# A rotary-embedding score kernel whose TensorE program becomes a loop, with explicit semaphores and whole stores

## The chip, the cores and the metric

The kernel runs on one core of a Trainium2 chip. The metric is the device time of one execution in microseconds (us); the time of a kernel is the median of its runs. A profile is one execution taken by the hardware profiler, and its span is a little shorter than the time (798.6 us here, for a time of 800.01 us).

A core has a matrix engine (TensorE, "PE" in the profile, with its weight loads as "PEld"), a vector engine (VectorE, "DVE"), a scalar engine (ScalarE, "ACT"), GpSimd ("POOL") and SyncE ("SP"), which here only issues transfers. Sixteen transfer (DMA) engines move data between the chip's memory (DRAM) and the core's on-chip memory. Matrix products land in PSUM and are copied from there by ScalarE or VectorE.

## The reference

Queries and keys of 16 batches, 512 positions, 16 heads and 64 dimensions are rotated by position, and then each head's scores are formed over all pairs of positions. All is float32.

```python
q, k: (16, 512, 16, 64);  cos, sin: (512, 32)

q1, q2 = q[..., :32], q[..., 32:]
q_rot = concatenate([q1 * cos - q2 * sin,  q1 * sin + q2 * cos], axis=-1)
# k_rot in the same way
scores = einsum('bshd,bthd->bsht', q_rot, k_rot)      # (16, 512, 16, 512)
```

The output has 268.4 MB, the inputs 67.1 MB: this kernel mostly writes.

## The kernel before

There are 64 steps, four for each batch. A step makes the scores of 128 query positions (one of four residues, `C = 4`) against all 512 key positions for the 16 heads, 4 MB, in a stage buffer `st` of which there are three, and stores it with one transfer.

In a step, eight score pairs (two heads each) go through TensorE into one of three PSUM buffers, and ScalarE evicts each pair into the stage buffer. Between them TensorE transposes rotated queries and keys of later steps through two PSUM banks, and VectorE does the rotation and half of the copies.

```python
    def scores(i, p, st):
        ps = ps_s_pool.tile([P, 2, S], fp32, tag="ps_s", name="ps")      # three buffers
        ...
        for r in range(2):
            po, rh = ps[:, r, :], rhs[64 * r : 64 * r + 64, :]
            nc.tensor.matmul(
                out=po, lhsT=lhs[64 * r : 64 * r + 64, :], rhs=rh, start=True, stop=True
            )
        ...
        nc.scalar.copy(out=so, in_=si)                                  # evicts into st
        ...
        elif b > 0 and p == HP - 1:
            store(i, st)
```

All stores but two are one transfer of 128 rows of 32 KB. Those of the steps 56 and 63 (`NST - 8` and `NST - 1`) are cut in three: most heads for all 128 rows, then the last two or three heads for 116 rows and for 12 rows.

```python
    def store(i, st):
        o = o_v[i // C, i % C]
        if i not in (NST - 8, NST - 1):
            nc.sync.dma_start(o, st)
            return

        h = H - 2 if i < NST - 1 else H - 3
        nc.sync.dma_start(o[:, :h], st[:, :h])
        nc.sync.dma_start(o[:116, h:], st[:116, h:])
        nc.sync.dma_start(o[116:, h:], st[116:, h:])
```

The main loop is a Python loop: every step's instructions stand in the program one by one. Waits between engines and for transfers are put in by the framework from the use of the tiles.

```python
        for i in range(C, NST):
            ...
            st = stage_pool.tile([P, H, S], fp32, tag="stage", name="st")
            for p in range(HP):
                scores(i, p, st)
                if p not in tr:
                    continue
                if tr[p][0] == "q":
                    run(dve[:1])
                    dve = dve[1:]
                    transposed(*tr[p], nc.vector.tensor_copy)
                else:
                    transposed(*tr[p], nc.scalar.copy)
            run(dve)
            if i % C == C - 2:
                load("q", i // C + 2)
            elif i % C == C - 1:
                load("k", i // C + 3)
```

The first four steps (`i < C`) are special: they work on batch 0 head by head, on inputs that come in four smaller loads into the third stage buffer (`early`), and store in pieces of 1 MB, so that the stores start early.

Of the kernel before, what the change touches and what calls it, by code (L numbers as in the profile page):

```python
# [7 lines left out]


@with_exitstack  # L10
def kernel(
# [15 lines left out]
    P = 128  # L27
# [3 lines left out]
    G = H // C  # L31

    const_pool = ctx.enter_context(tc.tile_pool(name="const", bufs=1))
    in_pool = ctx.enter_context(tc.tile_pool(name="in", bufs=2))
    part_pool = ctx.enter_context(tc.tile_pool(name="part", bufs=1))
    kt_pool = ctx.enter_context(tc.tile_pool(name="kt", bufs=2))
    qt_pool = ctx.enter_context(tc.tile_pool(name="qt", bufs=2))
    stage_pool = ctx.enter_context(tc.tile_pool(name="stage", bufs=3))
    ps_s_pool = ctx.enter_context(tc.psum_pool(name="ps_s", bufs=3))
    ps_t_pool = ctx.enter_context(tc.psum_pool(name="ps_t", bufs=2))  # L40

# [7 lines left out]
    ident = const_pool.tile([P, P], fp32, name="ident")  # L49
    cos_t = const_pool.tile([P, C, HD], fp32, name="cos_t")  # L50
    sin_t = const_pool.tile([P, C, HD], fp32, name="sin_t")
    ss_t = const_pool.tile([P, C, 2, HD], fp32, name="ss_t")
    ss_v = ss_t.rearrange("p c x j -> p c (x j)")

    st_first = [stage_pool.tile([P, H, S], fp32, tag="stage", name="st") for _ in range(2)]
    early = stage_pool.tile([P, 2 * C * H * D], fp32, tag="stage", name="early")
    units = {}
    used = [0]  # L60

    def load_units(which, head, heads):
        n = C * heads * D
        t = early[:, used[0] : used[0] + n].rearrange("p (c e) -> p c e", c=C)
        used[0] += n
        src = dram[which][0, :, :, head : head + heads, :]
        nc.sync.dma_start(t.rearrange("p c (h d) -> p c h d", d=D), src)
        for h in range(0, heads, G):
            units[which, (head + h) // G] = t[:, :, D * h : D * (h + G)]

    batches = {}

    def load(which, b):

        if b >= B:
            return
        t = in_pool.tile([P, C, H * D], fp32, tag=which + "_in", name=which + "_sb")
        batches[which, b] = t
        nc.sync.dma_start(t.rearrange("p c (h d) -> p c h d", h=H), dram[which][b])

    def rope(which, n):


        part = part_pool.tile([P, H * D], fp32, tag="part", name="part")
# [9 lines left out]
        else:  # L94
            x = batches[which, n // C][:, n % C]
# [7 lines left out]
        xs, xc = x.rearrange(sv, **k2), x.rearrange(sv, **k1)  # L103

        def products():
            nc.vector.tensor_tensor(pv, xs, ss, op=mult)  # L106
            nc.vector.tensor_tensor(xc, xc, cs, op=mult)  # L107

        def sums():
            for y, z in adds:  # L110
                nc.vector.tensor_tensor(y, y, z, op=add)  # L111
# [3 lines left out]
    kT = {}  # L115
    qT = {}

    def transposed(which, n, g, copy):


        bank = ps_t_pool.tile([P, 4, P], fp32, tag="ps_t", name="bank")
        for x in range(4):
            if n < C:
                src = units[which, n][:, x, P * g : P * (g + 1)]
            else:
                src = batches[which, n // C][:, n % C, P * (4 * g + x) : P * (4 * g + x + 1)]
            nc.tensor.transpose(bank[:, x, :], src, ident)  # L127
        src = bank
        if which == "q":
            if n not in qT:  # L130
                qT[n] = qt_pool.tile([P, HP, P], fp32, tag="qT", name="qT_t")
            dst = qT[n][:, 4 * g : 4 * g + 4, :]
        else:
            b = n // C
            if b not in kT:
                kT[b] = kt_pool.tile([P, HP, S], fp32, tag="kT", name="kT_t")
            if n < C:
                dst = kT[b][:, 2 * n + g].rearrange("p (t c) -> p t c", c=C)
                src = bank.rearrange("p c t -> p t c")
            else:  # L140
                dst = kT[b][:, 4 * g : 4 * g + 4, P * (n % C) : P * (n % C + 1)]
        copy(out=dst, in_=src)  # L142

    def store(i, st):
        o = o_v[i // C, i % C]
        if i not in (NST - 8, NST - 1):
            nc.sync.dma_start(o, st)
            return

        h = H - 2 if i < NST - 1 else H - 3  # L150
        nc.sync.dma_start(o[:, :h], st[:, :h])
        nc.sync.dma_start(o[:116, h:], st[:116, h:])
        nc.sync.dma_start(o[116:, h:], st[116:, h:])

    def scores(i, p, st):

        ps = ps_s_pool.tile([P, 2, S], fp32, tag="ps_s", name="ps")
        b = i // C
        if b == 0:
            c, hp = divmod(p, 2)  # L160
            lhs, rhs = qT[i][:, C * hp + c], kT[0][:, 2 * i + hp]
        else:
            lhs, rhs = qT[i][:, p], kT[b][:, p]
        for r in range(2):
            po, rh = ps[:, r, :], rhs[64 * r : 64 * r + 64, :]
            nc.tensor.matmul(  # L166
                out=po, lhsT=lhs[64 * r : 64 * r + 64, :], rhs=rh, start=True, stop=True
            )
# [4 lines left out]
        nc.scalar.copy(out=so, in_=si)  # L173
        if b == 0 and p % 2 == 1:
            c = p // 2
            nc.sync.dma_start(o_v[0, c, :, G * i : G * (i + 1)], st[:, G * c : G * (c + 1)])
        elif b > 0 and p == HP - 1:
            store(i, st)

    def tr_act(which, n):  # L180
        for g in range(2):
            transposed(which, n, g, nc.scalar.copy)
# [5 lines left out]
    with tc.manual_schedule():  # L188
        for t, src in ((cos_t, cos), (sin_t, sin)):
            nc.scalar.dma_start(t, src.rearrange("(p c) j -> p c j", c=C))  # L190
        for head, heads in ((0, G), (G, H - G)):
            load_units("k", head, heads)
            load_units("q", head, heads)
        load("k", 1)
        load("q", 1)
        make_identity(nc, ident)
        nc.scalar.copy(out=ss_t[:, :, 0, :], in_=sin_t)
        nc.scalar.mul(ss_t[:, :, 1, :], sin_t, -1.0)  # L198
        for which in ("k", "q"):
            run(rope(which, 0))  # L200
            tr_act(which, 0)


        for i in range(C):
            st = st_first[i] if i < 2 else stage_pool.tile([P, H, S], fp32, tag="stage", name="st")
            if i < C - 1:
                dve = rope("k", i + 1) + rope("q", i + 1) + rope("k", C + i)
                nxt = [("k", i + 1), ("q", i + 1)]
            else:
                dve = rope("q", C) + rope("k", C + i) + rope("q", C + 1) + rope("k", 2 * C)  # L210
                nxt = [("q", C), ("k", C + i)]
            for p in range(HP):
                scores(i, p, st)
                if p in (0, 1) and i > 0:
                    run(dve[:1])
                    dve = dve[1:]
                    transposed("k", C + i - 1, p, nc.vector.tensor_copy)
                if p == 3 and i < 2:
                    load("kq"[i], 2)
                if p in (2, 6):  # L220
                    m = len(dve) - (4 if p == 2 else 2) - (2 if i == C - 1 else 0)
                    run(dve[:m])
                    dve = dve[m:]
                    tr_act(*nxt.pop(0))
            run(dve)
        load("k", 3)


        for i in range(C, NST):
            tr = {}  # L230
            if i + 1 < NST:
                tr[1], tr[3] = ("q", i + 1, 0), ("q", i + 1, 1)
            if i + C < NST:
                tr[5], tr[6] = ("k", i + C, 0), ("k", i + C, 1)
            dve = []
            if i + 2 < NST:
                dve += rope("q", i + 2)
            if i + 1 + C < NST:
                dve += rope("k", i + 1 + C)
            st = stage_pool.tile([P, H, S], fp32, tag="stage", name="st")  # L240
            for p in range(HP):
                scores(i, p, st)
                if p not in tr:
                    continue
                if tr[p][0] == "q":
                    run(dve[:1])
                    dve = dve[1:]
                    transposed(*tr[p], nc.vector.tensor_copy)
                else:
                    transposed(*tr[p], nc.scalar.copy)  # L250
            run(dve)
            if i % C == C - 2:
                load("q", i // C + 2)
            elif i % C == C - 1:
                load("k", i // C + 3)
# [30 lines left out]
```

## Time and profile before

| what | value |
|---|---|
| time, median of 3 | 800.01 us (799.63 to 800.16) |
| span of the profile | 798.6 us |
| DRAM read, written | 67.24 MB, 268.44 MB |
| mean rate of the transfers | 421 GB/s |
| score matmuls | 2048 records, 653 ns mean |
| transposes (two rows of the profile) | 480 each, 308 and 287 ns mean |
| ScalarE eviction of a score pair | 512, 1019 ns mean |
| semaphore instructions on SyncE, ScalarE, VectorE, TensorE | 112, 78, 40, 32 |

A page of the profile gives the busy time of each engine, then the span in 40 equal slices with one digit for each (9 is busy for 90% or more), with the transfers' rate in GB/s below. Then the transfer queues: packets, MB and the share of the sixteen engines' time. Then the chain of waits that ended last, by engine and by line. Then groups of instructions: line, engine, operation, output<-inputs, count, busy us and mean ns, and after the second bar the idle time just before them with what ended it. Last, the issues of transfers, with the median us from issue to landing. The view of the waits names who waited for whom, with us in total, times, and the longest. Behind the page, the trace has a record for each packet that a transfer engine moved (start, duration, bytes, queue; not which engine) and for each landing (sixteen for a transfer on all engines).

### The profile page before, as it was taken

The page shows a single profiled execution, that of the slowest core. Times are in us where ns is not written, and L with a number is a line of the kernel's source. Part 1 is how long each engine was busy: PE and PEld are TensorE (multiplying, and loading weights), DVE is VectorE, ACT ScalarE, POOL GpSimd, SP SyncE. Part 2 cuts the span into 40 slices and gives each one's busy share as a digit, 9 for nine tenths or more (in the row PEclk, how much of TensorE's full clock was granted, in tenths as well). Part 3 has the DMA queues.
Part 4 walks back from the last instruction along what each step waited for, and adds up shares of the span by engine and source line. Part 5 has one row for each costly group of instructions (what it writes and reads, how often), then busy time and mean ns, then how long its engine had stood idle before and what let it go on. Part 6 is the DMA issues. An engine that isn't in the chain of part 4 may idle for free.

```text
span 798.6 us, 7719 instructions
## 1 busy us (share of the span) xinstructions
PE 690.1 (86%) x3072; PEld 299.2 (37%) x3072; DVE 544.5 (68%) x516; ACT 561.3 (70%) x647; POOL 0.7 (0%) x6
## 2 busy tenths in 40 slices
PE   4999998997979789797897988979889798899970
PEld 2444443433434334343343433424334243344420
DVE  7999987676857568575685766857758577586300
ACT  3888886776848668485785866858668586688770
POOL 0000000000000000000000000000000000000000
PEclk9999999899989899898998998999989899899995
DMA  9999999999999999999999999999999999999995
GB/s 357 421 411 435 437 423 433 423 427 440 421 431 429 429 437 427 436 421 434 426 432 434 431 420 429 434 429 437 427 424 407 443 422 440 423 404 419 426 426 235
DMA packets 17988, 336.17 MB, mean 421 GB/s; under 512 B 1824, under 2 KB 3104, under 8 KB 4384
## 3 DMA queue, kind: packets, MB, share of 16 engines
q1 hardware_dynamic: 17664, 335.55, 98.7%
q8 instruction: 24, 0.39, 0.2%
q10 hardware_dynamic: 288, 0.13, 0.1%
q14 instruction: 12, 0.10, 0.0%
HBM read 67.24 MB, written 268.44 MB: 420 GB/s over the span
## 4 chain that ended last, share of the span: by engine, by line
DMA 51%; PE 38%; ACT 4%; DVE 3%; issue 1%; ACTq 0%; SPq 0%
DMA out_dram<-st 48%; PE ps L166 29%; PE bank L127 9%; ACT st L173 4%; DMA q_sb<-in_q_dram 2%; DVE part L106 1%; DMA sin_t<-in_sin_dram 0%; DVE q_sb L107 0%; DVE k_sb L111 0%; DVE k_sb L107 0%; DVE q_sb L111 0%; DVE early L107 0%; DVE kT_t L142 0%; ACTq L281 0%; DVE early L111 0%
## 5 line engine op out<-in xcount | busy, mean ns | idle before, releaser
L173 ACT COPY st<-ps 128x1024 f32<-128x1024 f32 x512 | 495.0, 1019 | 203.4 <-DMA out_dram<-st 112.3
L166 PE MATMUL ps<-kT_t,qT_t 64*128 64x512 f32 x2048 | 547.9, 653 | 72.1 <-ACT st L173 72.1
L166 PEld LDWEIGHTS ps<-kT_t,qT_t 64*128 64x128 f32 x2048 | 185.0, 197 | 261.9 <-issue 140.6
L142 DVE COPY qT_t<-bank 128x512 f32<-128x512 f32 x118 | 81.5, 691 | 203.8 <-PE bank L127 203.8
L127 PEld LDWEIGHTS bank<-ident,q_sb 128*128 128x128 f32 x480 | 55.5, 151 | 102.4 <-issue 99.8
L127 PE MATMUL bank<-ident,q_sb 128*128 128x128 f32 x480 | 86.7, 308 | 0.9 <-PE ps L166 0.9
L127 PEld LDWEIGHTS bank<-ident,k_sb 128*128 128x128 f32 x480 | 50.5, 141 | 95.0 <-DVE k_sb L107 37.5
L127 PE MATMUL bank<-ident,k_sb 128*128 128x128 f32 x480 | 78.7, 287 | 1.2 <-DVE qT_t L142 1.2
L142 ACT COPY kT_t<-bank 128x512 f32<-128x512 f32 x122 | 72.5, 599 | 6.2 <-PE bank L127 6.2
L107 DVE TENSOR_TENSOR q_sb<-q_sb,cos_t 128x1024 f32<-128x1024 f32 x60 | 73.5, 1225 | 2.1
L111 DVE TENSOR_TENSOR k_sb<-k_sb,part 128x1024 f32<-128x1024 f32 x60 | 73.5, 1225 | 2.1
L107 DVE TENSOR_TENSOR k_sb<-k_sb,cos_t 128x1024 f32<-128x1024 f32 x60 | 73.5, 1225 | 2.0
L106 DVE TENSOR_TENSOR part<-q_sb,ss_t 128x1024 f32<-128x1024 f32 x60 | 73.5, 1225 | 2.0
L106 DVE TENSOR_TENSOR part<-k_sb,ss_t 128x1024 f32<-128x1024 f32 x60 | 73.0, 1216 | 0.1
L111 DVE TENSOR_TENSOR q_sb<-q_sb,part 128x1024 f32<-128x1024 f32 x60 | 72.9, 1216 | 0.0
L127 PE MATMUL bank<-ident,early 128*128 128x128 f32 x64 | 10.5, 316 | 12.3 <-DVE early L111 10.4
L127 PEld LDWEIGHTS bank<-ident,early 128*128 128x128 f32 x64 | 8.3, 161 | 17.3 <-issue 13.2
L106 DVE TENSOR_TENSOR part<-early,ss_t 128x1024 f32<-128x1024 f32 x8 | 9.8, 1223 | 5.7 <-ACT ss_t L198 5.5
L111 DVE TENSOR_TENSOR early<-early,part 128x512 f32<-128x512 f32 x16 | 10.3, 687 | 0.2
L107 DVE TENSOR_TENSOR early<-early,cos_t 128x1024 f32<-128x1024 f32 x8 | 9.8, 1225 | 0.3
L142 ACT COPY qT_t<-bank 128x512 f32<-128x512 f32 x10 | 5.7, 630 | 3.2 <-PE bank L127 3.2
L142 DVE COPY kT_t<-bank 128x512 f32<-128x512 f32 x6 | 4.1, 684 | 0.0
(9 smaller groups left out, 2.8 us busy)
## 6 DMA issues: line engine op xcount, KB each, us to landing
out_dram<-st SPq DMA_DIRECT2D x58, 4096.0 KB, 24.1
k_sb<-in_k_dram SPq DMA_DIRECT2D x15, 2048.0 KB, 27.6
q_sb<-in_q_dram SPq DMA_DIRECT2D x15, 2048.0 KB, 27.6
out_dram<-st SPq DMA_DIRECT2D x16, 1024.0 KB, 13.7
out_dram<-st SPq DMA_DIRECT2D x1, 3584.0 KB, 22.8
out_dram<-st SPq DMA_DIRECT2D x1, 3328.0 KB
early<-in_k_dram SPq DMA_DIRECT2D x1, 1536.0 KB, 8.8
early<-in_q_dram SPq DMA_DIRECT2D x1, 1536.0 KB, 12.0
```

The costliest lines, as they stand in the source:

```text
L106: nc.vector.tensor_tensor(pv, xs, ss, op=mult)
L107: nc.vector.tensor_tensor(xc, xc, cs, op=mult)
L111: nc.vector.tensor_tensor(y, y, z, op=add)
L127: nc.tensor.transpose(bank[:, x, :], src, ident)
L142: copy(out=dst, in_=src)
L166: nc.tensor.matmul(out=po, lhsT=lhs[64 * r : 64 * r + 64, :], rhs=rh, start=True, stop=True)
L173: nc.scalar.copy(out=so, in_=si)
```

## The change

TensorE's instructions for the steps 4 to 59 become a loop of seven turns, eight steps each. Eight steps are two batches, after which the double buffers of queries and keys stand as before, so the same instructions fit every turn. What differs between turns is only how far the other engines must have come: waits on ScalarE's and VectorE's counters. These are kept in two registers, which are raised by an addition ahead of each wait that needs another value. The other engines stay unrolled; only TensorE loops. The purpose is a TensorE program of about a quarter of its length, of which less has to be fetched from DRAM while the transfer engines are full.

The framework's automatic waits can't describe such a loop, so the kernel has its own planner: each operation is listed with what it reads and writes, `resolve` works out which counter value it must wait for, leaving out what is already known, and `emit` writes the instructions with explicit semaphores.

```diff
-from concourse.masks import make_identity
+class Plan:
+    def add(self, engine, emit, reads=(), writes=(), sem=None, also=()): ...
+    def resolve(self): ...                 # a wait for each operation, as few as possible
+    def emit(self, handles, first, period, turns):
...
+        for s in (ACT, DVE):
...
+            regs[s] = nc.tensor.alloc_register("wait_" + s)
+            nc.tensor.reg_mov(regs[s], vs[0])
+            now[s] = vs[0]
+        add = mybir.AluOpType.add
+        with nc.Fori(0, turns, engines=[mybir.EngineType.PE], hint_back_edge=False):
+            for m, op in enumerate(body[0]):
+                ws = list(waits[m].items())
+                for s, v in ws:
+                    if v != now[s]:
+                        nc.tensor.reg_alu(regs[s], regs[s], v - now[s], add)
+                        now[s] = v
...
+                a, b = op.emit()
+                for s, v in ws[:1]:
+                    a.wait_op(handles[s], regs[s], "sem-ge")
+                b.then_inc(handles[PE], 1)
+            for s in (ACT, DVE):
+                nc.tensor.reg_alu(regs[s], regs[s], low[s] + up[s] - now[s], add)
```

The score buffers in PSUM rotate through three, and eight steps have 64 score pairs, which three doesn't divide. So the last three pairs of a turn take the buffers 1, 2, 1 in place of 1, 2, 0:

```diff
+    def ps_of(i, p):
+        m = HP * i + p if i < FIRST else HP * ((i - FIRST) % PERIOD) + p
+        if i >= FIRST and m >= HP * PERIOD - 3:
+            return (1, 2, 1)[m - (HP * PERIOD - 3)]
+        return m % NPS
```

The cut stores are gone; every store is whole:

```diff
-    def store(i, st):
-        o = o_v[i // C, i % C]
-        if i not in (NST - 8, NST - 1):
-            nc.sync.dma_start(o, st)
-            return
-
-        h = H - 2 if i < NST - 1 else H - 3
-        nc.sync.dma_start(o[:, :h], st[:, :h])
-        nc.sync.dma_start(o[:116, h:], st[:116, h:])
-        nc.sync.dma_start(o[116:, h:], st[116:, h:])
...
         elif b > 0 and p == HP - 1:
-            store(i, st)
+            dma(SP, nc.sync, o_v[b, i % C], st, f"out{s}", reads=[("st", s, x) for x in range(HP)])
```

The whole program stands in a block with its own semaphores, which waits for all engines at its end and clears them:

```diff
-    with tc.manual_schedule():
+    plan.resolve()
+    with tc.tile_critical(), nc.cleanup_on_exit():
+        handles = {s: nc.alloc_semaphore(f"s_{s}") for s in plan.count}
+        plan.emit(handles, FIRST, PERIOD, TURNS)
+        nc.all_engine_barrier(sem_only=True)
```

The order of operations on each engine, the tiles and the amounts of data are otherwise those of before.

## The prediction

> **What bounds the kernel now.** I read the page from the top: busy shares, the slices, the queues, the chain of waits; then the waits of the store queue; then the packet and landing records of the trace behind the queue lines.
>
> ```profile
> PE 690.1 (86%) x3072; PEld 299.2 (37%) x3072; DVE 544.5 (68%) x516; ACT 561.3 (70%) x647; POOL 0.7 (0%) x6
> ...
> DMA  9999999999999999999999999999999999999995
> GB/s 357 421 411 435 437 423 433 423 427 440 421 431 429 429 437 427 436 421 434 426 432 434 431 420 429 434 429 437 427 424 407 443 422 440 423 404 419 426 426 235
> ...
> q1 hardware_dynamic: 17664, 335.55, 98.7%
> q8 instruction: 24, 0.39, 0.2%
> q10 hardware_dynamic: 288, 0.13, 0.1%
> q14 instruction: 12, 0.10, 0.0%
> ...
> DMA 51%; PE 38%; ACT 4%; DVE 3%; issue 1%; ACTq 0%; SPq 0%
> ...
> L173 ACT COPY st<-ps 128x1024 f32<-128x1024 f32 x512 | 495.0, 1019 | 203.4 <-DMA out_dram<-st 112.3
> ...
> out_dram<-st SPq DMA_DIRECT2D x58, 4096.0 KB, 24.1
> ```
>
> No engine is full, but the transfer engines are: 9 in every slice until the last. A store of 4096 KB takes 24.1 us from issue to landing, and ScalarE's largest wait is for a stage buffer whose store hasn't landed (112.3 us). So compute runs ahead of the stores and waits for them. The small queues tell one more thing: q8 moved 24 packets of together 0.39 MB, 16,384 bytes each. TensorE ran 3072 matmul records and 3072 weight loads, 6144 instructions; 6144/24 = 256 instructions of 64 bytes. q8 is TensorE's instruction fetch, one block for every 256 instructions.
>
> ```profile
> SPq L147 <- ACT st L173: 645.8, 58, 16.3
> SPq L176 <- ACT st L173: 48.7, 16, 14.2
> SPq L281 <- DMA out_dram<-st: 17.8, 1, 17.8
> ```
>
> This is the store queue's own wait list: 17.8 us of the end is nothing but the last store landing.
>
> How far ahead is compute? In the timeline ScalarE, which waited for a stage buffer to land, resumes at 437.77 us and fills it and the next one; the second of the two stores is issued at 458.51 us: 20.7 us for two steps, 10.4 us a step. A batch (four stores, two loads) takes 49.3 us, 12.3 us a step. TensorE and ScalarE have 1.9 us of slack in every step.
>
> The packet records say more. A 32,768-byte row takes a transfer engine 1213 ns, so eight rows and a completion write are 9.68 us a store. Each store has sixteen landings, one per engine. How late the second slowest and the slowest engine land after the first one, in us:
>
> ```
> store whose first landing is at   301.78  501.27  698.11  779.26
> second slowest engine              4.49    6.24    5.56    2.94
> slowest engine                     7.01   10.61   11.76    9.37
> ```
>
> One engine, the same throughout, falls steadily behind: its landings are 9.95 us apart in back-to-back stores, not 9.68. Its store packets take 1227 to 1274 ns, never 1213; its load packets are normal. This one engine, call it F, is the bound: it never lacks work (a store's issue lies some 14 us, 24.1 - 9.95, ahead of F's first packet of it) and the whole program ends when F has moved its sixteenth of the bytes. The chain's 51% DMA is F.
>
> The two split stores of before (steps 56 and 63) are fitted to F. In the records the 116-row parts run on four engines, 29 packets each, the 12-row parts on twelve engines, one packet each; so F gives up most of its share, and F and those four engines end together: their last packets end between 796.7 and 797.1 us, the other engines' by about 789 us.
>
> [...]
>
> **The change part by part.**
>
> 1. TensorE's loop. 512 matmul instructions stand in the program instead of 2048. In records: 232 matmuls before the loop, 384 in it, 152 after it, each with a weight load, so 464, 768 and 304 instructions; with 78 register additions and the branch the body is about 850, 3.3 blocks, and the whole some 1,650, 6.4 blocks. If the loop stays resident, fetches fall from 24 to about 6 or fewer. What is that worth? The fetches rotate over the engines (the disturbed engine is another each time, with a packet of 1580 to 1630 ns beside it), and F's landings show only two, of the fetches at 207.8 and 735.5 us: 10.57 and 10.71 us instead of about 9.95, some 0.6 and 0.75 us, together 1.35 us. So removing the fetch's 24 packets takes 1.35 us from F and nothing else that sets the end.
>
> 2. Register additions and waits: 78 a turn, 546 in all, about ten a step. If each cost as much as the shortest operation in the timeline, a memset of 0.10 us, and none were hidden, that is 1.0 us a step, below the 1.9 us of slack. Seven turns are six backward branches; even if each had to fetch its block and TensorE stood still for 4 us (an estimate: the first sine load, issued at 1.14 us, took 3.80 us until it landed), F's 14 us lead and 8 x 1.9 = 15 us of slack in a turn cover it. Cost on the path: 0.
>
> 3. Explicit semaphores: SyncE's semaphore instructions fall from 112 to 10, TensorE's from 32 to 12; ScalarE's stay (78, now 79). SyncE mostly waits for ScalarE anyway (645.8 us). 0.
>
> 4. The third score buffer is skipped at a turn's end (order 1, 2, 1): one score pair waits for an eviction of 1.02 us, within the slack. 0.
>
> 5. Whole stores. F gets its share back. Step 56: 8 x (1213 - 1062) - 159 = 1.05 us. Step 63: 8 x (1213 - 987) - 234 = 1.57 us. Sum 2.62 us more for F. Against it, F's last two packets beside the split parts took 1449 and 1204 ns instead of 987, 0.68 us that should go.
>
> 6. Entry and exit. The block with its own semaphores adds a wait at entry and, at exit, a clear of semaphores and about three barriers. The first barrier of before shows as 0.29 us of idle on GpSimd. Four of them: about +1.2 us.
>
> Sum: F's end 797.0 + 2.62 - 0.68 - 1.35 = 797.6 us; before, the span ends 1.5 us after the last packet (798.6 - 797.1); 797.6 + 1.5 + 1.2 = 800.3 us span, 1.7 more than before. Time: 800.0 + 1.7 = 801.7 us; I say 801.5.
>
> **The rivals.**
>
> A. F's slowness is not the engine's own but comes with something the change removes. Then the second slowest engine sets the end: without splits the undisturbed engines end at 787.2 + 3.0 = 790.2 us, the second slowest 2.9 us later, 793.1; with 2.7 us after it the span is 795.8 and the time 797. For it: the splits were dropped. Against: F is slow on its stores from 90 us on, uniformly, with fetches or without.
>
> B. The loop doesn't stay resident: each turn fetches its 3 to 4 blocks again, 27 to 33 fetches instead of 24. F keeps its two or gets a third: 1.35 to 2.1 us above the sum, 803 to 804 us. [...] q8's line will tell.
>
> C. TensorE becomes the bound: if each register wait delays its weight loads by over 1.9/12 = 0.16 us, a step exceeds 12.3 us. At 0.25 us it would be 13.4 us, 64 steps, some 860 us. Against it: now the weight loads wait 140.6 us in 621 pieces of at most 0.5 us for nothing the profile shows, so instructions already trickle in without harm.
>
> D. The fetches all mattered (24 x 1.3 us = 31 us, as if on F). The landings refute it: F shows two.
>
> **Range and chances.** Main line with or without B: 800 to 804. A gives 797. Eight in ten: 797 to 806. Over 2% faster needs 784 us, below even A: 0.02. Over 2% slower needs 816 us, only C: 0.04. Within 2%: 0.94.
>
> **What would show it.** q8's packets: about 6 if resident, about 30 if not. F still slow: last landings 9.95 us apart in back-to-back stores, lag over 10 us at 700 us. The last packet near 797.6 us, on one engine, the others done by about 793. SyncE's last wait near 18 us or more. TensorE's busy time near 690 us. I am wrong if the lag of the slowest engine is near that of the second (A), or if ScalarE's wait for landings shrinks from 112.3 us while its wait for TensorE (76.4 us) grows and the DMA row has 8s (C).

## Result, and the profile after

The changed kernel takes 804.2 us (median of 4 runs, 803.79 to 807.26), beside 799.8 us for the kernel before in the same series: ratio 1.0065, 95% interval 1.0047 to 1.0082. It is slower by some 5 us (4.4 us by the two medians). That is within 2% and inside the predicted range, but 2.7 us above the predicted 801.5.

The page of the changed kernel, the lines that answer to those shown of before:

```profile
PE 688.5 (86%) x3072; PEld 298.0 (37%) x3072; DVE 545.2 (68%) x516; ACT 562.5 (70%) x647; POOL 0.7 (0%) x6
...
DMA  9999999999999999999999999999999999998994
GB/s 347 419 425 435 432 414 426 427 433 433 426 430 432 427 439 417 441 425 439 428 430 434 431 432 426 437 430 423 426 428 407 433 412 420 429 434 358 419 439 199
...
q1 hardware_dynamic: 17376, 335.55, 98.3%
q10 hardware_dynamic: 288, 0.13, 0.1%
q8 instruction: 6, 0.10, 0.0%
q14 instruction: 11, 0.09, 0.0%
...
DMA 48%; PE 38%; DVE 6%; ACT 5%; issue 0%; ACTq 0%; DVEq 0%; SPq 0%
...
L373 ACT COPY st<-ps 128x1024 f32<-128x1024 f32 x512 | 495.6, 1018 | 203.1 <-DMA out_dram<-st 102.4
...
out_dram<-st SPq DMA_DIRECT2D x60, 4096.0 KB, 24.7
```

q8, TensorE's fetches, fell from 24 packets to 6. The packet records have them at 34, 61, 93, 115, 147 and 763 us: none stands between 147 and 763 us, while the loop of 3.3 blocks branched back six times (148.5 to 645.5 us). It was not fetched again. The engines are as busy as before, the transfers move the same bytes, the DMA row is full but for one slice near 730 us (358 GB/s). So the 3.9 us that the span grew by are in no compute engine's busy time; they are small delays of the transfers.

The waits of the store queue and of ScalarE in the changed kernel (who waits, for whom: us, times, longest):

```profile
SPq L229 <- ACT st L373: 722.3, 76, 15.8
SPq L116 <- DMA out_dram<-st: 20.2, 1, 20.2
...
ACT st L373 <- DMA out_dram<-st: 102.4, 27, 6.2
ACT st L373 <- PE ps L364: 86.7, 128, 2.3
```

ScalarE waits 10 us less for landings and 10 us more for TensorE, where before it was 112.3 and 76.4. This is the shift that the prediction named as a sign of TensorE becoming the bound. It is not that: the first and the eighth eviction of a step start 9.11 us apart (median) in the looped and in the unrolled kernels alike. A wait in front of a buffer that isn't free yet has only changed its name: the two together are 188.7 us before and 189.1 us after.

Where the time went can be read from the slow engine F, whose store packets, mostly of 1227 to 1274 ns, give it away in the packet records. The table has the moment at which it ends four stores or its last landing, in us, for one profiled run of each kernel. (e2 and e9 are experiments below: before with whole stores; after with TensorE unrolled.)

```
                              before     e2      e9   after
F ends a store near 109 us     109.2   108.7   109.3   108.8
the store near 159 us          158.7   158.1   159.9   159.4
the store near 740 us          738.8   738.9   740.3   740.8
last landing                   797.5   799.0   799.8   800.3
end of the span                798.6   799.8   801.8   802.5
```

Before to after, stretch by stretch: 109 to 159 us takes 50.6 instead of 49.5 (+1.1); 159 to 740 takes 581.4 instead of 580.1 (+1.3); from there to the last landing 59.5 instead of 58.7 (+0.8); after the last landing 2.1 instead of 1.1 (+1.0); before 109 us -0.4. Sum +3.8 of the span's 3.9.

The windows of the end, before and then after (stretch, its length, busy us of PE, PEld, DVE, ACT and POOL with their counts, clock, DMA share, GB/s):

```profile
720.00:740.00 20.00, 18.95 (x91) 8.43 (x92) 12.08 (x12) 18.00 (x21) 0.00 (x0) 1.00 0.98 413
```

```profile
720.00:740.00 20.00, 17.45 (x78) 7.70 (x80) 12.29 (x12) 15.61 (x18) 0.00 (x0) 0.91 0.83 357
```

Once the loads are over, the fast engines run dry for the first time (DMA share 0.83): F lags 12 us behind them (12.4 us between the first and the last landing of the store that lands from 728.87 us on), and its buffers aren't free in time (ScalarE waits 3.9 us for a landing there). They have nothing to lose by it, since F ends last anyway. A dip in the DMA row need not be a loss.

### The profile page after: what moved, and what is told of

It is laid out like the page before. It is cut to its first block, busy times and chain, and to the rows that moved or that the text cites. A ratio compares the mean times of both kernels' runs of the same rounds, so it can differ in the third digit from the quotient of the medians.

```text
span 802.5 us, 8182 instructions
## 1 busy us (share of the span) xinstructions
PE 688.5 (86%) x3072; PEld 298.0 (37%) x3072; DVE 545.2 (68%) x516; ACT 562.5 (70%) x647; POOL 0.7 (0%) x6
## 4 chain that ended last, share of the span: by engine, by line
DMA 48%; PE 38%; DVE 6%; ACT 5%; issue 0%; ACTq 0%; DVEq 0%; SPq 0%
DMA out_dram<-st 47%; PE ps L364 28%; PE bank L315 9%; ACT st L373 5%; DVE part L290 2%; DVE st L290 2%; DVE k_sb L290 1%; DVE q_sb L290 1%; DMA st<-in_k_dram 1%; DVE kT L333 0%; DVE qT L333 0%; ACTq L103 0%; DVEq L103 0%; SPq L497 0%; SPq L468 0%
## 5 line engine op out<-in xcount | busy, mean ns | idle before, releaser
L364 PE MATMUL ps<-kT,qT 64*128 64x512 f32 x2048 | 545.8, 649 | 74.7 <-ACT st L373 74.7
L364 PEld LDWEIGHTS ps<-kT,qT 64*128 64x128 f32 x2048 | 183.7, 196 | 265.0 <-issue 137.6
L333 DVE COPY qT<-bank 128x512 f32<-128x512 f32 x118 | 81.5, 691 | 202.8 <-PE bank L315 202.8
L333 ACT COPY kT<-bank 128x512 f32<-128x512 f32 x122 | 72.6, 598 | 6.8 <-PE bank L315 6.8
L315 PE MATMUL bank<-ident,st 128*128 128x128 f32 x64 | 10.7, 318 | 13.3 <-DVE st L290 13.3
L315 PEld LDWEIGHTS bank<-ident,st 128*128 128x128 f32 x64 | 8.3, 161 | 18.5 <-DVE st L290 16.8
L290 DVE TENSOR_TENSOR part<-st,ss_t 128x1024 f32<-128x1024 f32 x8 | 9.8, 1223 | 6.4 <-DMA st<-in_k_dram 6.1
L290 DVE TENSOR_TENSOR st<-st,part 128x512 f32<-128x512 f32 x16 | 11.1, 691 | 0.5
L290 DVE TENSOR_TENSOR st<-st,cos_t 128x1024 f32<-128x1024 f32 x8 | 9.8, 1225 | 0.3
L333 ACT COPY qT<-bank 128x512 f32<-128x512 f32 x10 | 5.7, 617 | 3.5 <-PE bank L315 3.5
## 6 DMA issues: line engine op xcount, KB each, us to landing
st<-in_q_dram SPq DMA_DIRECT2D x1, 1536.0 KB, 12.4
```

Source lines behind the costliest of these rows:

```text
L290: plan.add(DVE, one(lambda: nc.vector.tensor_tensor(o, a, b, op=op)), reads, writes, also=more)
L315: done = [nc.tensor.transpose(bank[:, x, :], srcs[x], ident) for x in range(4)]
L333: plan.add(engine, one(lambda: copy(out=dst, in_=src)), [("bank", m)], keys)
L364: nc.tensor.matmul(out=ps[:, r, :], lhsT=lhs[lo:hi, :], rhs=rhs[lo:hi, :], start=True, stop=True)
```

## First series: which part costs what

Four kernels, each compared with the kernel before in the same series (800.83 us there).

**e1: the cut stores put back into the changed kernel.**

```diff
+            if i not in (NST - 8, NST - 1): (whole store, as in the change)
+            else: three stores as in the kernel before: [:, :h], [:116, h:], [116:, h:]
```

> The changed kernel with the two cut stores of before put back, and nothing else. Theory (the slowest transfer engine F sets the end, and whole stores cost it some 2.6 us): 801.0 to 802.2 us against 804.2 of the changed kernel; F's last landing some 2.0 to 3.3 us earlier. Rival 1 (TensorE's loop with its register waits costs the time): no difference, 804. Rival 2 (the explicit semaphores with their entry and exit cost it all): 804.

Measured: 803.88 us (22 runs), ratio 1.0041, interval 1.0029 to 1.0053. The theory's range is missed by 1.7 us: with loop, planner and the old stores, 3 us remain.

**e2: the kernel before with whole stores.**

```diff
-        if i not in (NST - 8, NST - 1):
-            nc.sync.dma_start(o, st)
-            return
... (and the three cut stores)
+        nc.sync.dma_start(o_v[i // C, i % C], st)
```

> The kernel before with whole stores, and nothing else. Theory: 802.0 to 802.8 us, before plus 2.0 to 2.6 us. Rivals 1 and 2: 800, as before.

Measured: 801.35 us (14 runs), ratio 1.0009, interval 0.9997 to 1.0021. The rival is nearer: by the ratio whole stores cost about 0.7 us, not 1.9, and the interval reaches from nothing to 1.7 us.

**e3: the changed kernel with TensorE written out**, whole stores kept.

```diff
-        with nc.Fori(0, turns, engines=[mybir.EngineType.PE], hint_back_edge=False):
-            ... (registers, body, and the steps before and after it)
+        for op in pe:
+            plain(op)
```

> The changed kernel with TensorE's program written out instead of looped, waits on constants, everything else as in it. Theory: 804.2 to 805.6 us: as the changed kernel, or up to 1.35 us slower for the fetches that hit F; 24 packets on the fetch queue again. Rival 1: 801.3 us (before plus 1.25 us of entry and exit). Rival 2: 804.

Measured: 802.86 us (22 runs), ratio 1.0022, interval 1.0014 to 1.0030. Its q8 line has 24 packets again. The theory said that it loses 1.35 us by that and comes out at 804 or more; instead it beats the looped kernels.

**e4: the planner alone**: unrolled as e3, cut stores as e1.

> TensorE written out and the cut stores put back: only the planner's explicit semaphores with the block's entry and exit remain of the change. Theory: before plus the 1.25 us that entry and exit show in the traces, 801.0 to 801.8 us. Rival 1: the same. Rival 2: 804.

Measured: 802.2 us (22 runs), ratio 1.0013, interval 1.0003 to 1.0023: by the ratio, the planner with its block costs 1.0 us; by the medians 1.4 us, and the median lies 0.4 us above the expected range. The four ratios give three differences: planner, entry and exit 0.13%; whole stores 0.09% (e2 over before, and e3 over e4); the loop 0.28% (e1 over e4), plus or minus 0.16, which is 2.2 us by the ratios and 1.7 us by the medians. The loop, the part that was to save, costs most.

What the traces of this series showed: in the looped kernels the load packets are disturbed more. Their 16,384 bytes take 611 ns; summed over all engines from 200 to 700 us, what they took beyond that was 23 to 39 us in the unrolled kernels (before, e2, e3, e4) and 55 and 89 us in the looped ones (after, e1; the profiled run of e1 was its longest, so its 89 is high). The excess comes in bursts. Some five to ten store packets that began within 0.2 us of each other, the last of their store before a load, take 0.5 to 1.2 us longer; 5 us later a score of load packets take 0.4 to 1 us longer each. Below, the first of the two is called a jam.

## Second series: what of the loop?

Before in this series: 800.02 us.

**e5: the changed kernel again.**

> The changed kernel once more, as the measure for the three kernels beside it. All theories: 803.5 to 805.5 us, 0.4 to 0.7% over the kernel before; 6 fetch packets of TensorE; the 16 KB load packets between 200 and 700 us take over 50 us more, summed over the sixteen engines, than at their usual length, where the unrolled kernels show 23 to 28 us. If it comes out within 0.2% of the kernel before, what was read as the loop's cost was scatter from one program load to the next.

Measured: 804.87 us (6 runs), ratio 1.0057, interval 1.0038 to 1.0076. Load excess 64 us. The loss is repeatable.

**e6: the loop body written out seven times**, register additions and register waits kept.

```diff
-        with nc.Fori(0, turns, engines=[mybir.EngineType.PE], hint_back_edge=False):
-            for m, op in enumerate(body[0]):
+        for turn in range(turns):
+            for m, op in enumerate(body[turn]):
```

> The loop body written out seven times, its register additions and its waits on register values kept, the branch gone. Theory 1 (the loop's 2 to 3 us come from the loads' packets, and those are disturbed only where the looped program runs): about 802.7 us, 0.2% over the kernel before, some 27 fetch packets, load excess 20 to 30 us. Rival (register waits delay TensorE and with it the stores): as the loop, 804 to 805 us, 0.4 to 0.6% over.

Measured: 803.77 us (5 runs), ratio 1.0045, interval 1.0032 to 1.0059; load excess 48 us, between the groups. It lies between the looped kernels of this series (1.0049, 1.0057) and the unrolled ones (e3 1.0022, and e9 below 1.0027), and its interval reaches the first. So the branch and the missing fetches aren't needed for most of the loss, if the medians are taken at their word; five runs don't separate it from either.

**e7: the loop, with six copies of its matmuls behind a branch that is never taken**, so that the program is as large as the unrolled one.

```diff
+        never = nc.tensor.alloc_register("never")
+        nc.tensor.reg_mov(never, 1)
+        with nc.tensor.If_eq(never, 0):
+            for t in range(1, turns):
+                for op in body[t]:
+                    op.emit()
```

> The changed kernel with six more copies of the loop body's matmuls at the end of TensorE's program, behind a branch that is never taken: the program is as large as the unrolled one, what runs is the loop. Rival (the size of the program decides where things lie in memory, and that is the difference): as the unrolled kernels, about 802.7 us, 0.2% over the kernel before, load excess 20 to 30 us. Theory (what is run decides, not what is loaded): as the loop, 804 to 805 us, 0.4 to 0.6% over, load excess over 50 us, 6 to 8 fetch packets.

Measured: 804.22 us (5 runs), ratio 1.0049, interval 1.0035 to 1.0063; load excess 58 us. What was loaded with the program made no difference (1.0049 beside e5's 1.0057); what ran did (e3's 1.0022). The fetch lines of e6 and then e7, from the queue part of their pages:

```profile
q8 instruction: 26, 0.43, 0.2%
```

```profile
q8 instruction: 8, 0.13, 0.1%
```

**e8: the kernel before with five cut stores of another shape**, meant to take load from F and beat both kernels.

```diff
-        if i not in (NST - 8, NST - 1):
+        if i not in (12, 24, 36, 48, 60):
...
-        h = H - 2 if i < NST - 1 else H - 3
+        h = H - 2
-        (rows :116 and 116:)
+        (rows :119 and 119:)
```

> The kernel before, with five cut stores (steps 12, 24, 36, 48, 60) instead of two; the last two heads go as 119 rows [...] and 9 rows [...]. Each cut takes 8 x (1213 - 1062) - 159 = 1.05 us from the slow engine, five take 5.2 us, and give seven other engines 17 x 151 - 8 x 151 = 1.36 us each, 6.8 us in all. If the slow engine alone sets the end: its end moves from 797.1 (2.6 us of which the two old cuts had saved) to about 794.5 us, the seven end at about 787 + 7 = 794; 797.5 to 798.5 us, 0.3% under the kernel before. Rival (an engine's freed time is lost elsewhere, as in the run with whole stores, where 2.6 us more for the slow engine cost 0.7 us): no gain, within 0.1%.

Measured: 816.54 us (6 runs), ratio 1.0204, interval 1.0177 to 1.0231: a miss by 18 us, in the other direction. Its store rows (queue, count, KB each, median us from issue to landing) show what a cut store does:

```profile
out_dram<-st SPq DMA_DIRECT2D x55, 4096.0 KB, 25.1
...
out_dram<-st SPq DMA_DIRECT2D x5, 3584.0 KB, 30.2
```

The smaller part lands later than a whole store. And F wasn't relieved but loaded: it ends the same stores 0.5 us ahead of e3 at 158 us, 3.1 us behind at 261 us and 5.8 us behind at 462 us, after two of the cuts. That is 3.1 us a cut, where 17 rows in place of its share of eight make 17 x 159 - 8 x 151 = 1.5 us (most packets of 4 KB took 159 ns). F's packets show that it got 17 of the 119 rows: at the cut of step 24 its eight packets of 28 KB are followed by 17 of 4 KB, which end at 343.07 us. The expectation had given it one row. These 17 took 3.8 us instead of 2.7, single ones up to 0.67 us; where the rest of the 3.1 us lies stays open. Of the old parts of 12 rows F moved one packet and of the 116 rows none; that it would stay out of the 119 too was the author's estimate, and it failed. Other engines ran ahead and dry: in 740 to 760 us the DMA share was 0.90, and in the store that lands from 753 us on thirteen of sixteen landings lie within 0.18 us. There were six jams from 200 to 703 us, as defined above, where the kernel before has one.

## Third series: are the jams the cause?

Before in this series: 800.23 us. At this point the theory was: the fetches of an unrolled TensorE delay one engine or another and so keep the sixteen apart; without them they end their stores together, jam, and the loads collide.

**e9: the unrolled kernel again (as e3), and e12: the changed kernel a third time**, on one chip.

> The unrolled kernel with whole stores once more, on the same chip as the three beside it, so that the loop's own part is read without a change of chip. If the loop itself costs 2 us or more: about 802.5 us, 0.2% over the kernel before, 0.3% or more under the looped kernel of this call. If what was read as the loop's cost came with the chip: within 0.15% of it. Moments in which five or more store packets that began together all take over 250 ns too long (called a jam below): one, as in the earlier profile of it, where the looped kernels had two to five.

> The changed kernel a third time, as the measure for the three beside it: 803.5 to 805.5 us, 0.45 to 0.65% over the kernel before, two jams or more, load excess over 50 us.

Measured: e9 802.87 us (8 runs), ratio 1.0027, interval 1.0016 to 1.0039; e12 804.97 us (5 runs), ratio 1.0052, interval 1.0038 to 1.0066. Side by side the loop costs 2.1 us, 0.25% plus or minus 0.18. Load excess 40 and 58 us; jams two and three.

**e10: the changed kernel with one store cut into steps**, meant to spread the moments at which the engines end their stores. How many rows of each part an engine moves was the author's estimate.

```diff
+            if i == 5:  (all but the last four heads whole; the last four in row groups,
+                         in this order)
+                for rows in (34, 15, 14, 13, 12, 11, 10, 9, 8, 2): ...
```

> The changed kernel, with one store (step 5) cut [...] Theory (engines that finish their stores together jam at the switch to the loads, and the loads after it collide; that is where the looped kernel loses its time): fewer jams than two, load excess under 40 us, 801.5 to 803 us, 0.2 to 0.4% over. Rival (jams follow from something else, such as the time within the run): jams and time as in the looped kernel, 804 to 805 us.

Measured: 807.24 us (5 runs), ratio 1.0082, interval 1.0068 to 1.0096. The cut itself costs: the windows of e10 and then of e12 at that place,

```profile
80.00:100.00 20.00, 20.00 (x99) 8.82 (x98) 18.25 (x18) 17.33 (x21) 0.00 (x0) 1.00 0.92 383
100.00:120.00 20.00, 20.00 (x97) 8.84 (x96) 17.10 (x16) 17.11 (x21) 0.00 (x0) 1.00 0.96 369
```

```profile
80.00:100.00 20.00, 20.00 (x98) 8.82 (x100) 18.17 (x19) 17.34 (x21) 0.00 (x0) 1.00 0.99 426
100.00:120.00 20.00, 20.00 (x98) 8.82 (x98) 17.08 (x16) 17.34 (x21) 0.00 (x0) 1.00 1.02 410
```

that is, (426 - 383 + 410 - 369) x 20 us = 1.68 MB not moved, 4 us of the whole rate, and F ends the store near 159 us at 163.0 instead of 160.9 us. After that came what the cut was meant to bring: no jam from 112 to 611 us, load excess 42 instead of 58 us. How far apart the engines ran was not shown. And it gained nothing. From its store near 159 us to the one near 740 us F took 581.6 us, as in the looped kernels (after 581.4, e5 582.0, e7 581.5, e12 581.1), not as in the unrolled ones with whole stores (e2 580.8, e3 580.4, e9 580.4; e6, with register additions and no branch, 580.8). Both sides missed the time; the theory falls in the point that matters: fewer jams didn't make F faster.

**e11: the changed kernel with fetches brought back on GpSimd**, twenty lots of 256 small memsets.

```diff
+        if p == 0 and i >= 5 and i % 3 == 2:
+            plan.add(POOL, fill, [("tick", i, p)], ["spare"])
+    def fill():
+        done = [nc.gpsimd.memset(spare[:, x : x + 1], 0.0) for x in range(256)]
```

> The changed kernel, with twenty lots of 256 small memsets on GpSimd, so that instructions are fetched again, about as often as by the unrolled TensorE (20 to 40 packets). Theory (fetches push the transfer engines apart and keep them from jamming): 801.5 to 803 us, 0.2 to 0.4% over, load excess under 40 us. Rival (fetches only cost, and the looped kernel's loss has another cause): 804.5 to 806 us, as the looped kernel or worse.

Measured: 815.03 us (5 runs), ratio 1.0178, interval 1.0164 to 1.0192, 10 us above e12. Neither had that. The busy row and the two fetch queues (q14 has 11 packets in the changed kernel):

```profile
PE 693.1 (85%) x3072; PEld 298.6 (37%) x3072; DVE 545.3 (67%) x516; ACT 563.2 (69%) x647; POOL 171.8 (21%) x5126
...
q14 instruction: 51, 0.42, 0.1%
...
q8 instruction: 6, 0.10, 0.0%
```

5120 memsets made 40 more packets (51 - 11) of 8,192 bytes, two for each lot. F does lose time with each lot: 17 lots start after 170 us, and with each of them one of its stores takes 0.57 to 0.95 us more than 9.68 us, where its other stores take some 0.28 us more:

```
lot of memsets, us     177-187  213-223  252-261  293-301  328-337  364-374  403-414  443-453
a store of F ends at    191.2    226.4    261.8    302.0    342.0    377.2    412.5    452.6
over 9.68 us by          0.57     0.76     0.95     0.85     0.63     0.79     0.80     0.77
```

But it isn't the fetches that F pays for. From 195 to 640 us, over eleven whole lots, F's packets follow one another without a gap, and none of the lots' fetches stands among them: those ran on other engines. (The one q14 packet on F, at 479.13 us, is one that e12 has too, at 474.39.) What changes is F's own store packets. During the lot of 213 to 223 us six of them take 1312 to 1364 ns, while nearly all of the other engines' packets beside them keep to 1213. How long a store packet of F takes goes with the number of instructions, of all engines of the core, that end while it is moved:

```
instructions ended during the packet   0-1   8-9  12-13  16-17  20-21   40 or more (e11)
F's store packet, mean ns             1218  1232   1245   1254   1262   1336
```

The first five columns are from ten kernels (before, after, e2 to e7, e9, e12; 143 to 700 us, packets over 1300 ns left out), the last from e11, with 53 instructions on average. A straight line through the points of each of these eleven kernels rises by 2.2 to 2.5 ns for each instruction. At 2.2 ns, the 256 memsets of a lot make 0.56 us; the 17 stores exceed F's others by 0.77 - 0.28 = 0.49 us on average. Twenty lots at some 0.5 us are the 10 us.

So the run doesn't test whether fetches spread the engines. It shows what makes F slow: not a fetch, but instructions. Where next to none end, F is nearly as fast as the others (1218 beside 1213 ns), and its load packets don't grow with them (median 611 ns). Whether it is the instruction or its record in the profile that slows F, no run here separates.

## Why the prediction was right, and where it wasn't

The time came within 0.4% of what was said and lies in the stated range, and the bound was the one named: F ends last in the kernels with whole stores, at some 9.95 us a store, with or without fetches. The change itself was mis-sized: 1.7 us in the sum, 4.4 us measured (5 by the ratio). A range of 797 to 806 us was wide enough for both, so that it holds says little for the sum. Step by step:

1. The loop. Six fetches as said. "Removing the fetch's 24 packets takes 1.35 us from F" is the step that failed: F got nothing back (159 to 740 us took it 0.6 us more than in e2, 1.0 more than in e9), and the looped kernels are 2.1 us slower than the unrolled ones (e12 and e9; 1.7 us by e1 and e4). The two long landings from which the 1.35 us were read stood beside fetches of TensorE, and were put down to them by nearness in time. The packet records of before show what hit F there: two packets of q14, of 8,192 bytes, at 204.76 and 734.47 us, 0.32 us each, both ahead of TensorE's fetch and each followed by a long store packet (1539 and 1508 ns). No fetch of TensorE stands among F's packets from 159 to 700 us, in before, e2, e3, e4, e9 or after.

2. Register additions. One takes 32 ns on TensorE (median of the 546 in after), the backward branch 0.21 us (0.208 to 0.233 us, six in after). The first weight load of a turn starts 0.94 us after the one before it, in the looped kernels (after, e12) and in the unrolled ones (e3, e9) alike, and the step's 9.11 us is unchanged. So "cost on the path: 0" holds for compute, but not for F. Over the same 336 store packets from 159 us on, F needs 10.3 to 10.5 us more than 1213 ns each in before, e3, e4 and e9 (11.0 in e2), and 11.1 to 11.5 us more in the kernels with register additions (after, e5, e6, e7, e12). The looped kernel ends 564 instructions more than the unrolled e3 (8182 and 7618), 546 of them these additions; at 2.4 ns each, for the four fifths of the time in which F stores, that is 1.1 us. It is an estimate from one profiled run of each kernel, and the kinds of instruction were not tried one by one, but it fits e6 too, which has the additions without the loop.

3. Semaphores, and 6, entry and exit. Predicted 0 and +1.2 us; e4 measures both together as 1.0 us. In the profile the first load is issued 0.22 us later (the two timelines, before and then after):

```profile
0.73 0.66 SPq L67 DMA_DIRECT2D early<-in_k_dram  x1
```

```profile
0.95 0.67 SPq L229 DMA_DIRECT2D st<-in_k_dram  x1
```

and 1.03 us more lie behind the last landing: 1.25 us. But F also loses some 1 us from 109 to 159 us in nearly all kernels of the planner (50.6 us after and e9, 50.7 e4, 51.2 e12, but 49.9 e3; 49.5 in before and 49.4 in e2), loop or none, beside a burst of long load packets near 111 us. The prediction had no such term.

4. The order 1, 2, 1 of the score buffers wasn't tried by itself; e3 and e4 have it too, so it is part of the planner's 1.0 us.

5. Whole stores. Predicted 2.62 - 0.68 = +1.9 us; e2 over before and e3 over e4 both give 0.7 us by the ratios, and neither interval excludes 0 or 1.7. On F's clock (e2 against before) it is 2.1 us: 0.7 from 159 to 740 us and 1.4 after it, where one of the two q14 packets has moved from the first stretch to the second. So what F has to move was sized rightly; why the time grew by less stays open.

So the sum fell about 2 us short. The saving of 1.35 us isn't there, the register additions cost F about 1 us by the estimate above, where 0 was said, and 1 us in the start-up of the planner's schedule had no term. Against that stand a start that came 0.4 us earlier in the profiled run, one q14 packet fewer on F, and, by the times, whole stores that cost some 1 us less than said.

Rivals: A is refuted as it stands (F stays slow without the fetches), and the prediction's "never 1213" as well: in before, 57 of F's 356 store packets from 143 to 700 us take 1213 to 1223 ns, those in which few instructions end. F's slowness does come with something, the instructions, but the change brings more of them, 8182 for 7719. B is refuted by q8's 6; C by the unchanged step, though its sign, the shifted wait, was seen; D because no fetch of TensorE stands among F's packets.

What stays open is the other half of the loop's 2 us. Shown: it is not the program's size (e7), not a slower step, and not by way of the jams (e10). What e6, with 1.0045, leaves to the branch is within the scatter. No version of the study beats the kernel before.

## What to carry to other kernels

When transfers are the bound, find the engine that ends last and charge a change by what that one engine gets or loses: TensorE's eighteen fetches fewer were worth nothing, since none was found on F; 5120 small memsets, which no other engine waits for, cost 10 us. A delay that lies near an event in time need not come from it: follow the one engine's packets and see what stands between them, before a saving goes into a sum. And measure the scaffolding apart from the idea: here planner, entry and exit cost about 1 us before the loop had done anything.

## What the runs showed of the hardware

- A TensorE loop of about 850 instructions (an estimate: 3.3 blocks of 16,384 bytes) was fetched once for its seven turns: 6 packets for the whole program, none between 147 and 763 us. Its six backward branches over these blocks took 0.21 to 0.23 us each.
- The 5120 memsets on GpSimd (e11) brought 40 more fetch packets of 8,192 bytes, one for every 128.
- The store packets of one of the sixteen transfer engines lengthened by 2.2 to 2.5 ns for each instruction that ended on the core meanwhile (eleven kernels): 1218 ns with none or one, 1254 with 16 or 17, 1336 with some 53. Nearly all store packets of the other engines kept to 1213 ns (98% of them up to 1214 ns in before and in after, 143 to 700 us), and this engine's load packets to some 611 (median, before and after).
- In the jams, five to ten store packets that began within 0.2 us of each other, the last of their store before a load, took up to 2.4 us instead of 1.21 us (2.42 us in e12, 2.38 us in after, 2.39 us in before).
- Cutting a store in the middle of the run cost far more than its packets: 2.1 us for the slow engine in e10 and 3.1 us for each cut in e8, where its packets at their usual lengths make 1.5 us. At the end of the run (the kernel before) it may pay: some 0.7 us, with intervals that reach nothing.
